# A two-layer decoder trunk on one core: a sixth pair of chunks by seven products, two chunks set aside, SiLU as one activation

## The chip, the core and the metric

The kernel runs on one core of one Trainium2 chip. The time is device microseconds of one execution. The program is written in a language in which every instruction is placed on an engine: PE (TensorE, matrix products), DVE (VectorE), ACT (ScalarE), POOL (GpSimd) and SP (SyncE, which here only issues transfers). Each engine runs its own instructions in the order in which the program lists them and waits on semaphores for the others.

## The reference

Two decoder layers over 256 tokens of width 1024. A layer is a token mixer and a SwiGLU sublayer, each followed by a residual and a layer norm. The change touches the second sublayer alone:

```python
D_FF = -(-8 * D_MODEL // (3 * 256)) * 256        # 2816

def swiglu(x, w_gate, w_up, w_down):
    return (jax.nn.silu(x @ w_gate) * (x @ w_up)) @ w_down

def reference(x, ...):
    for l in range(DEPTH):
        mix = hybrid_mixer(x, w_in[l], w_branch_sb[l], w_branch_moba[l], w_out[l])
        x = layer_norm(DEEPNORM_ALPHA * x + mix, ln_mix_g[l], ln_mix_b[l])
        ffn = swiglu(x, w_ffn_gate[l], w_ffn_up[l], w_ffn_down[l])
        x = layer_norm(DEEPNORM_ALPHA * x + ffn, ln_ffn_g[l], ln_ffn_b[l])
    return x
```

All inputs are float32.

## The kernel before

**Three products for one.** Every matrix is split into a high part of type float32r and a low part, the remainder. A product is `hi*hi + hi*lo + lo*hi`, three matrix instructions into one accumulator (`mm3`, L455; the instruction itself is recorded under L449). The weights come from memory in granules of 128x1024 float32 (512 KB). SP loads a granule into one of six `raw` tiles, ACT casts it into the ring `whi` (`CAST whi<-raw`, recorded under L57, the helper `act`), and DVE subtracts to get `wlo` (`TENSOR_TENSOR wlo<-raw,whi`, under L62, the helper `dve`). Both rings hold ten granules, so a granule can be split only once PE has used the one ten places ahead. In the mixer five granules a layer come by another way (`dma_line`, L183): POOL issues a load straight into `whi` (L187), ACT writes its negative into `wlo`, and POOL issues a second load that adds the weights onto it (L194).

**The second sublayer.** Its 2816 hidden features are 22 chunks of 128, numbered 0 to 21. Chunks 0 to 3 are made token by token (`h_line`, tiles `l0pft`, `l0sg`), and 4 to 21 feature by feature (`swiglu_line`, tiles `l0pf`, `l0sf`): ACT takes the sigmoid of the gate, DVE multiplies it by the gate and then by the other half, and the result is split into `h_hi` and `h_lo`. Then comes the down projection, whose stage the tiles `l0pd`, `l0ps`, `l0pt` (layer 1: `l1pd`, `l1pe`, `l1pt`) mark. For one chunk it takes a weight granule of 128x1024 and forms two token tiles by two halves of 512 columns: four results of three products each, 12 instructions.

**Pairs by seven products.** Two chunks together are a 2x2 block product, which the kernel does in the Strassen-Winograd way: seven products of blocks (21 instructions) in place of eight. For that, sums of the activations (`sums_line`: four additions on DVE of 128x128, then a split) and sums of the weights are needed. In the stream of weights a pair (p, q) is four steps: b (the granule of q, split whole), a (the granule of p, of which only the first half is split), then four sums of 128x512 that DVE makes in place in the two raw tiles, and t and u, which are these sums, each split whole. A chunk that is not in a pair is one step n. Accumulators `one`, `six`, `five`, `seven` (the tiles `ps` and `pt`; in layer 1 `ps` is a part of `pd`) collect products over all pairs; `combine_line` (L1070) afterwards adds them into the residual tiles x0 and x1 with eight DVE operations.

**What sets the order.** A planner in Python (`Weave`) keeps an estimate of each engine's time while the program is written, and lets side lines (splits, activations, norms) issue their next step when they are due. `DOWN` gives the order of chunks and pairs in the down projection. Its last eight entries (`HOLD`) are done for token tile 0 first, then for token tile 1, so that the norm of tile 0 can run beside the products of tile 1. `ASIDE` names chunks whose weights do not go through the rings: `put_aside` gives them a place in `xT_hi` and `xT_lo`, the transposed x, which is free once the last gate product has read it, and loads them there as `dma_line` does, except that the negative is made by POOL. Before, `ASIDE` is empty. The planner's entry for that POOL instruction is 0.3 us and a further 2.7.

Of the kernel before, what the change touches and what calls it, by code (L numbers as in the profile page):

```python
# [14 lines left out]
P = 128  # L15
DEPTH = 2
D = 1024
S = 256
# [10 lines left out]
NEG = -1e30  # L29
GCOLS = 1024  # L30
NG_LAYER = 122
DOWN = ((0, (4, 5), (6, 7), 1, (8, 9), 2, (10, 11), 3, (12, 13), 14, 15, 16, 17, 18, 19, 20, 21),
        (0, (4, 5), (6, 7), 1, (8, 9), 2, (10, 11), 3, (12, 13), 14, 15, 16, 17, 18, 19, 20, 21))
STEPS = [[e for d in down for e in
          ([("n", d)] if isinstance(d, int) else [("b", d[1]), ("a", d[0]), ("t", d[0]), ("u", d[0])])]
         for down in DOWN]
# [238 lines left out]
START = (("x00", 4.4), ("x10", 5.4), ("x01", 6.4), ("w10", 6.4), ("w11", 7.4), ("x11", 7.4), ("w20", 8.2), ("x02", 9.0),  # L275
         ("w21", 9.7), ("x12", 10.3), ("w30", 11.0), ("w31", 11.7))
BY_DMA = ((18, 23, 28, 33, 38), (18, 23, 28, 33, 38))
ASIDE = ((), ())
X_AFTER = {(2, 0): (0, 2), (2, 1): (1, 2)}
NSPLIT = 10  # L280
HOLD = 8
# [41 lines left out]
def hybrid_trunk_kernel(ctx: ExitStack, tc: tile.TileContext, w, xT_in, x_in, ln_in,  # L323
# [144 lines left out]
    def pe_done():  # L468
        return weave.t + HOP
# [336 lines left out]
    for l in range(DEPTH):  # L806
# [130 lines left out]

        def h_line(name, ps, j, t):
            sg = small_work(name, [P, 256])
            e = act(pe_done(), 256, nc.scalar.activation, sg, ps[:, :256], AF.Sigmoid)  # L940
            yield e
            dve(e, 256, nc.vector.tensor_mul, sg, sg, ps[:, :256])
            e = dve(e, 256, nc.vector.tensor_mul, sg, sg, ps[:, 256:])
            yield e + MARGIN
            tp = bankC(name + "T", [P, 2, P])
            pe_after(e)
            for i in range(2):
                transpose(tp[:, i, :], sg[:, i * P:(i + 1) * P])
            ts = slice(t * P, (t + 1) * P)
            e = pe_done()  # L950
            yield e
            yield from split_line(h_t[0][0][:, 2 * j:2 * j + 2, ts], h_t[0][1][:, 2 * j:2 * j + 2, ts], tp, 256, e)
# [5 lines left out]
        def sums_line(i, e):  # L958

            a, b = (raw_h.pop(c) for c in pairs[i])  # L960
            (a0, a1), (b0, b1) = ([x[:, t * P:(t + 1) * P] for t in range(2)] for x in (a, b))
            tmp = small_work(f"{L}hs{i}", [P, 4, P])
            for j, x, y, op in ((0, b1, a1, OP.subtract), (1, a0, tmp[:, 0], OP.add), (2, a0, a1, OP.subtract),
                                (3, b0, tmp[:, 1], OP.subtract)):
                e = dve(e, P, nc.vector.tensor_tensor, tmp[:, j], x, y, op=op)
            if i < 2:
                both = wide_work(f"{L}hw{i}", F32R).rearrange("p a h c -> p (a h c)")[:, :GCOLS]
            elif i < 4:
                both = work.tile([P, 2, 2, S], F32R, tag=("sbq", "sbk")[i - 2],
                                 name=f"{L}hw{i}").rearrange("p a h c -> p (a h c)")  # L970
            if i < 4:
                sums[i] = [both[:, n * 512:(n + 1) * 512].rearrange("p (j c) -> p j c", c=P) for n in range(2)]
            else:
                sums[i] = [x[:, 2:, :].rearrange("p k (j c) -> p (k j) c", c=P) for x in h_t[-1]]
            yield e
            yield from split_line(*sums[i], tmp, 512, e)

        def swiglu_line(name, ps, hi, lo, c):
            sg = small_work(name, [P, S])
            e = act(pe_done(), S, nc.scalar.activation, sg, ps[:, 0, :], AF.Sigmoid)  # L980
            yield e
            dve(e, S, nc.vector.tensor_mul, sg, sg, ps[:, 0, :])
            e = dve(e, S, nc.vector.tensor_mul, sg, sg, ps[:, 1, :])
            yield e
            if c in pair_of:
                i = pair_of[c]
                raw_h[c] = sg
                n = P if c == pairs[i][0] else S
                e = yield from split_line(hi[:, :n], lo[:, :n], sg[:, :n], n, e)
                if n == S:  # L990
                    yield from sums_line(i, e)
                return
            yield from split_line(hi, lo, sg, S, e)
# [53 lines left out]
        def seven_products(i, g):  # L1047

            a, b = pairs[i]
            (b_hi, b_lo), (a_hi, a_lo) = ws.take(g), ws.take(g + 1)  # L1050
            t0, t1 = slice(0, P), slice(P, S)
            one_, two_ = slice(0, 512), slice(512, GCOLS)
            (ha, la), (hb, lb) = h_parts(a), h_parts(b)
            s_hi, s_lo = sums[i]
            last = i == len(pairs) - 1
            into(c11, hb[:, t0], lb[:, t0], b_hi[:, one_], b_lo[:, one_])
            into(c12, s_hi[:, 3], s_lo[:, 3], b_hi[:, two_], b_lo[:, two_])
            ws.used(g)
            into(one, ha[:, t0], la[:, t0], a_hi[:, one_], a_lo[:, one_], last)
            ws.used(g + 1)  # L1060
            m_hi, m_lo = ws.take(g + 2)
            into(five, s_hi[:, 0], s_lo[:, 0], m_hi[:, one_], m_lo[:, one_], last)
            into(seven, s_hi[:, 2], s_lo[:, 2], m_hi[:, two_], m_lo[:, two_], last)
            ws.used(g + 2)
            m_hi, m_lo = ws.take(g + 3)
            into(six, s_hi[:, 1], s_lo[:, 1], m_hi[:, two_], m_lo[:, two_], last)
            into(c21, hb[:, t1], lb[:, t1], m_hi[:, one_], m_lo[:, one_])
            ws.used(g + 3)

        def combine_line(e):  # L1070

            v, r = (small_work(f"{L}{n}", [P, 512]) for n in ("pv", "pr"))
            x0, x1 = xs
            e = act(e, 512, nc.scalar.copy, v, six)
            yield e
            e = dve(e, 512, nc.vector.tensor_sub, v, one, v)
            residual(e, x0, halves[0], one)
            e = dve(e, 512, nc.vector.tensor_add, r, seven, v)
            e = dve(e, 512, nc.vector.tensor_add, v, five, v)
            residual(e, x0, halves[1], v, op=OP.subtract)  # L1080
            residual(e, x1, halves[0], r)
            e = dve(e, 512, nc.vector.tensor_add, r, five, r)
            residual(e, x1, halves[1], r, op=OP.subtract)

        g = G + NG_LAYER - NFC
        at = {}
        for n, d in enumerate(DOWN[l][:-HOLD]):
            if n == 6:
                late()
            if isinstance(d, int):  # L1090
                for t in range(2):
                    chunk(banks[t], g, d, t)
                ws.used(g)
                g += 1
                continue
            i = pairs.index(d)
            while i not in sums:
                weave.finish(swiglus)
            seven_products(i, g)
            g += 4  # L1100
            if i == len(pairs) - 1:
                combine = weave.start(combine_line(pe_done()))
        norms = []
        for t in range(2):
            def down(part, c0=NFC - HOLD, c1=NFC, first=False, last=True, t=t):
                for c in range(c0, c1):
                    chunk(part, g + c - NFC + HOLD, c, t, first and c == c0, last and c == NFC - 1)
                    if t == 1:
                        ws.used(g + c - NFC + HOLD)
                weave.finish([combine])  # L1110
# [91 lines left out]
```

## Time and profile before

| | before |
|---|---|
| runs, us | 720.8, 721.76 and a first one of 4118.94; median 721.76 |
| the profiled execution, us | 720.93 |
| its span, us | 719.2 |
| PE busy, share of the span | 710.8 us, 99% |
| DVE busy | 581.6 us, 81% |
| ACT busy | 407.9 us, 57% |
| POOL busy | 29.3 us, 4% |
| read from memory | 139.69 MB, 196 GB/s over the span |
| mean granted TensorE clock | 0.998 |

The span runs from the first to the last instruction of the program. A row of the timeline gives the start, the duration, the engine, the line of the kernel, the operation with its output and inputs (tile names without their numbers), and in brackets the idle time before it with what ended it. In a row of several instructions (x5) the duration is that of all together. A row of the list of waits gives who waited for whom.

### The profile page before, as it was taken

Reading aid. Unit: us, or ns where it says so; the run is one execution under the profiler, and the core shown is the slowest. Engines: PE = TensorE matmul, PEld = TensorE weight load, DVE = VectorE, ACT = ScalarE, POOL = GpSimd, SP = SyncE. Lnnn points to the kernel's source line nnn. Section 1 sums busy time; section 2 is a strip of 40 time slices with the busy share of each in tenths; the row PEclk is TensorE's granted clock in tenths of the full one; section 3 lists DMA queues with packets and bytes.
Section 4 is the critical chain, followed back from the end, with each engine's and each line's share of the span. In section 5 each row is a group of like instructions: output and inputs, shape, how many; then the busy total and the mean of one; then the engine's idle time right before and its main releaser. Section 6 shows DMA issues by size and latency. Waiting matters only on the chain.

```text
span 719.2 us, 12730 instructions
## 1 busy us (share of the span) xinstructions
PE 710.8 (99%) x5002; PEld 653.6 (91%) x5002; DVE 581.6 (81%) x871; ACT 407.9 (57%) x618; POOL 29.3 (4%) x50
## 2 busy tenths in 40 slices
PE   9999999999999999999999999999999999999995
PEld 7998999998899999988889989999888999998885
DVE  5988776698888777799877897778778877778986
ACT  6855676655565554557357557675446655544530
POOL 0000010000000000000000001000010000000001
PEclk9999999999999999999999999999999999999999
DMA  8986664367586564349459637636846865524731
GB/s 326 378 251 199 158 196 108 127 247 265 187 277 224 188 197 145 126 157 345 162 177 309 185 93 206 206 102 210 269 152 204 280 190 201 189 97 130 238 113 58
DMA packets 40668, 141.57 MB, mean 197 GB/s; under 512 B 4640, under 2 KB 5664, under 8 KB 40608
## 3 DMA queue, kind: packets, MB, share of 16 engines
q1 hardware_dynamic: 37152, 129.75, 53.6%
q0 software_dynamic: 2880, 10.49, 6.7%
q8 instruction: 39, 0.64, 0.3%
q10 hardware_dynamic: 576, 0.52, 0.2%
q14 instruction: 21, 0.17, 0.1%
HBM read 139.69 MB, written 1.05 MB: 196 GB/s over the span
## 4 chain that ended last, share of the span: by engine, by line
PE 99%; DVE 0%; POOL 0%; POOLq 0%; DVEq 0%; issue 0%
PE l1pf L449 14%; PE l0pf L449 14%; PE l0pg L449 6%; PE l1pg L449 6%; PE l0pd L449 6%; PE l1pd L449 4%; PE l0pk L449 3%; PE l1pk L449 3%; PE l0pq L449 3%; PE l0pft L449 3%; PE l1pft L449 3%; PE l1pvq L449 3%; PE l1pw L449 3%; PE l0pw L449 3%; PE l1pb L449 3%; PE l0pb L449 3%
## 5 line engine op out<-in xcount | busy, mean ns | idle before, releaser
L62 DVE TENSOR_TENSOR wlo<-raw,whi 128x1024 fp32r<-128x1024 f32 (+1 forms) x256 | 299.3, 1189 | 31.8 <-ACT whi L57 28.6
L57 ACT CAST whi<-raw 128x1024 fp32r<-128x1024 f32 (+1 forms) x256 | 256.9, 1023 | 60.9 <-DVE raw L62 25.0
L449 PE MATMUL l0pf<-xT_hi,whi 128*128 128x256 f32 x288 | 79.6, 276 | 0.0
L449 PE MATMUL l1pf<-xT_hi,whi 128*128 128x256 f32 x288 | 79.6, 276 | 0.0
L449 PE MATMUL l0pf<-xT_lo,whi 128*128 128x256 f32 x288 | 79.5, 276 | 0.0
L449 PE MATMUL l0pf<-xT_hi,wlo 128*128 128x256 f32 x288 | 79.5, 276 | 0.0
L449 PE MATMUL l1pf<-xT_lo,whi 128*128 128x256 f32 x288 | 79.5, 276 | 0.0
L449 PE MATMUL l1pf<-xT_hi,wlo 128*128 128x256 f32 x288 | 79.5, 276 | 0.0
L449 PEld LDWEIGHTS l1pf<-xT_lo,whi 128*128 128x128 f32 x288 | 54.1, 188 | 0.0
L449 PEld LDWEIGHTS l0pf<-xT_lo,whi 128*128 128x128 f32 x288 | 54.1, 188 | 0.0
L449 PEld LDWEIGHTS l0pf<-xT_hi,whi 128*128 128x128 f32 x288 | 54.1, 188 | 0.0
L449 PEld LDWEIGHTS l1pf<-xT_hi,whi 128*128 128x128 f32 x288 | 54.1, 188 | 0.0
L449 PEld LDWEIGHTS l0pf<-xT_hi,wlo 128*128 128x128 f32 x288 | 54.1, 188 | 0.0
L449 PEld LDWEIGHTS l1pf<-xT_hi,wlo 128*128 128x128 f32 x288 | 54.1, 188 | 0.0
L449 PE MATMUL l0pg<-xT_hi,whi 128*128 128x256 f32 x128 | 35.6, 279 | 0.0
L449 PE MATMUL l1pg<-xT_hi,whi 128*128 128x256 f32 x128 | 35.6, 278 | 0.0
L449 PE MATMUL l0pg<-xT_lo,whi 128*128 128x256 f32 x128 | 35.4, 276 | 0.0
L449 PE MATMUL l0pg<-xT_hi,wlo 128*128 128x256 f32 x128 | 35.4, 276 | 0.0
L449 PE MATMUL l1pg<-xT_lo,whi 128*128 128x256 f32 x128 | 35.4, 276 | 0.0
L449 PE MATMUL l1pg<-xT_hi,wlo 128*128 128x256 f32 x128 | 35.4, 276 | 0.0
L62 DVE TENSOR_TENSOR l1sf<-l1sf,l1pf 128x256 f32<-128x256 f32 x36 | 15.1, 421 | 15.4 <-ACT l1sf L57 14.7
L62 DVE TENSOR_TENSOR l0sf<-l0sf,l0pf 128x256 f32<-128x256 f32 x36 | 15.1, 421 | 11.9 <-ACT l0sf L57 11.2
(475 smaller groups left out, 1838.2 us busy)
## 6 DMA issues: line engine op xcount, KB each, us to landing
raw<-in_w_dram SPq DMA_DIRECT2D x230, 512.0 KB, 4.3
whi<-in_w_dram POOLq DMA_DIRECT2D x10, 512.0 KB, 4.3
wlo<-in_w_dram POOLq DMA_DIRECT2D x10, 512.0 KB, 7.2
ln<-in_ln_dram SPq DMA_DIRECT2D x8, 512.0 KB, 6.2
raw<-in_w_dram SPq DMA_DIRECT2D x8, 256.0 KB, 4.6
x<-in_x_dram SPq DMA_DIRECT2D x2, 512.0 KB, 8.2
out_dram<-x SPq DMA_DIRECT2D x3, 256.0 KB, 2.0
xT_raw<-in_xT_dram ACTq DMA_DIRECT2D x4, 128.0 KB, 4.5
```

What stands on the lines that cost most here:

```text
L57: f(*args, **kw)
L62: f(*args, **kw)
L449: nc.tensor.matmul(o, a, b, start=start, stop=stop)
```

## The change

The change has five parts, all in the second sublayer.

- `DOWN`: six pairs a layer in place of five; (14, 15) is new. The order changes too: five pairs stand first, then chunk 0, the sixth pair, chunk 1, and for the last eight chunks 2, 3 and 16 to 21, where it was 14 to 21.
- `ASIDE`: the weights of chunks 16 and 17 are loaded into the place of the transposed x.
- SiLU: one activation `Silu` on ACT, where it was a sigmoid on ACT and a multiplication on DVE.
- `sums_line`: a place for the sixth pair's sums (in free halves of the tiles of `h`).
- `combine_line`: its eight operations are issued in four pieces with at least 3.2 us of the planner's time between them. The ln parameters of the second norm are loaded one entry earlier (`n == 5`).

```diff
-DOWN = ((0, (4, 5), (6, 7), 1, (8, 9), 2, (10, 11), 3, (12, 13), 14, 15, 16, 17, 18, 19, 20, 21),
+DOWN = (((4, 5), (6, 7), (8, 9), (10, 11), (12, 13), 0, (14, 15), 1, 2, 3, 16, 17, 18, 19, 20, 21),
...
-ASIDE = ((), ())
+ASIDE = ((16, 17), (16, 17))
...
         def h_line(name, ps, j, t):
             sg = small_work(name, [P, 256])
-            e = act(pe_done(), 256, nc.scalar.activation, sg, ps[:, :256], AF.Sigmoid)
+            e = act(pe_done(), 256, nc.scalar.activation, sg, ps[:, :256], AF.Silu)
             yield e
-            dve(e, 256, nc.vector.tensor_mul, sg, sg, ps[:, :256])
             e = dve(e, 256, nc.vector.tensor_mul, sg, sg, ps[:, 256:])
...
             if i < 4:
-                sums[i] = [both[:, n * 512:(n + 1) * 512].rearrange("p (j c) -> p j c", c=P) for n in range(2)]
+                places = [[both[:, n * 512:(n + 1) * 512].rearrange("p (j c) -> p j c", c=P) for n in range(2)]]
+            elif i == 4:
+                places = [[x[:, 2:, :].rearrange("p k (j c) -> p (k j) c", c=P) for x in h_t[-1]]]
+            elif i == 5:
+                places = [[x[:, 0::2, P:] for x in h_t[k]] for k in (1, 2)]
             else:
-                sums[i] = [x[:, 2:, :].rearrange("p k (j c) -> p (k j) c", c=P) for x in h_t[-1]]
+                places = [[x[:, 6:, :].rearrange("p k (j c) -> p (k j) c", c=P) for x in (xT_hi, xT_lo)]]
+            n = 4 // len(places)
+            sums[i] = [[hi_lo[m][:, j] for hi_lo in places for j in range(n)] for m in range(2)]
             yield e
-            yield from split_line(*sums[i], tmp, 512, e)
+            for k, hi_lo in enumerate(places):
+                e = yield from split_line(*hi_lo, tmp[:, k * n:(k + 1) * n], n * P, e)
 
         def swiglu_line(name, ps, hi, lo, c):
             sg = small_work(name, [P, S])
-            e = act(pe_done(), S, nc.scalar.activation, sg, ps[:, 0, :], AF.Sigmoid)
+            e = act(pe_done(), S, nc.scalar.activation, sg, ps[:, 0, :], AF.Silu)
             yield e
-            dve(e, S, nc.vector.tensor_mul, sg, sg, ps[:, 0, :])
             e = dve(e, S, nc.vector.tensor_mul, sg, sg, ps[:, 1, :])
...
             e = dve(e, 512, nc.vector.tensor_sub, v, one, v)
             residual(e, x0, halves[0], one)
+            yield weave.t + 3.2
             e = dve(e, 512, nc.vector.tensor_add, r, seven, v)
             e = dve(e, 512, nc.vector.tensor_add, v, five, v)
+            yield weave.t + 3.2
             residual(e, x0, halves[1], v, op=OP.subtract)
             residual(e, x1, halves[0], r)
+            yield weave.t + 3.2
             e = dve(e, 512, nc.vector.tensor_add, r, five, r)
             residual(e, x1, halves[1], r, op=OP.subtract)
...
-            if n == 6:
+            if n == 5:
                 late()
...
-                    chunk(part, g + c - NFC + HOLD, c, t, first and c == c0, last and c == NFC - 1)
+                    chunk(part, g + c - NFC + HOLD, DOWN[l][c - NFC], t, first and c == c0, last and c == NFC - 1)
```

The order of the instructions at three places follows. On DVE in layer 0's down stage, a raw tile's number is the step's number in the stream of weights. Before, from the t of the pair (8, 9) to the t of the pair (10, 11):

```order
L62 TENSOR_TENSOR wlo_91<-raw111_3297,whi_89 128x1024
L62 TENSOR_TENSOR wlo_91<-raw110_3173,whi_89 128x1024
L62 TENSOR_TENSOR wlo_91<-raw114_3299,whi_89 128x1024
L62 TENSOR_TENSOR wlo_91<-raw115_3423,whi_89 128x1024
L62 TENSOR_TENSOR wlo_91<-raw116_3425,whi_89 128x512
L62 TENSOR_TENSOR raw116_3425<-raw116_3425 128x512
L62 TENSOR_TENSOR raw116_3425<-raw116_3425,raw115_3423 128x512
L62 TENSOR_TENSOR raw115_3423<-raw115_3423,raw116_3425 128x512
L62 TENSOR_TENSOR raw115_3423<-raw115_3423 128x512
L62 TENSOR_TENSOR wlo_91<-raw116_3425,whi_89 128x1024
```

Now, on the same engine, from the t of the pair (10, 11) to the t of the pair (12, 13):

```order
L62 TENSOR_TENSOR wlo_91<-raw113_3273,whi_89 128x1024
L62 TENSOR_TENSOR wlo_91<-raw112_3271,whi_89 128x1024
L62 TENSOR_TENSOR wlo_91<-raw116_3395,whi_89 128x1024
L62 TENSOR_TENSOR wlo_91<-raw117_3397,whi_89 128x512
L62 TENSOR_TENSOR raw117_3397<-raw117_3397 128x512
L62 TENSOR_TENSOR raw117_3397<-raw117_3397,raw116_3395 128x512
L62 TENSOR_TENSOR raw116_3395<-raw116_3395,raw117_3397 128x512
L62 TENSOR_TENSOR raw116_3395<-raw116_3395 128x512
L62 TENSOR_TENSOR wlo_91<-raw117_3397,whi_89 128x1024
```

The whole split of the plain chunk (raw114) that stood between two pairs is gone from this place; one pair's t and u are followed at once by the next pair's b and a.

On POOL, between the first norm of layer 0 (`l0a_ve`) and its second (`l0b_ve`), as one piece of the difference:

```order
 L67 TENSOR_TENSOR l0a_ve_2061<-l0a_ve_2061,few 128x1
-L67 TENSOR_SCALAR l0b_ve_3775<-l0b_ve_3775 128x1
-L67 TENSOR_TENSOR l0b_ve_3775<-l0b_ve_3775,few 128x1
-L67 TENSOR_SCALAR l0b_ve_3866<-l0b_ve_3866 128x1
-L67 TENSOR_TENSOR l0b_ve_3866<-l0b_ve_3866,few 128x1
+L187 DMA xT_hi<-in_w_dram 128x1024 x2
+L67 TENSOR_SCALAR xT_lo<-xT_hi 128x1024 x2
+L194 DMA xT_lo<-in_w_dram 128x1024 x2
+L67 TENSOR_SCALAR l0b_ve_3765<-l0b_ve_3765 128x1
+L67 TENSOR_TENSOR l0b_ve_3765<-l0b_ve_3765,few 128x1
```

Six instructions are new on POOL's queue: two loads, two multiplications of 128x1024 by -1, and two adding loads.

On ACT in layer 1, at the first activation of the second sublayer (`l1sg00`, which reads the gate product `l1pft00`), before:

```order
L57 CAST whi_89<-raw193_5647 128x1024
L57 ACTIVATE l1pw1_5700,l1a_ve1_5781<-x1_88,l1a_nmu1_5780 128x1024
L57 ACTIVATE l1sg00_5829<-l1pft00_5804 128x256
L57 CAST whi_89<-raw194_5657 128x1024
L57 CAST xT_hi_85<-l1a_tp10_5838 128x4x128
L57 CAST whi_89<-raw195_5664 128x1024
```

And now:

```order
L57 CAST whi_89<-raw195_5637 128x1024
L57 ACTIVATE l1pw1_5690,l1a_ve1_5771<-x1_88,l1a_nmu1_5770 128x1024
L57 ACT_TABLE_LOAD
L57 ACTIVATE l1sg00_5819<-l1pft00_5794 128x256
L57 CAST whi_89<-raw196_5647 128x1024
L57 CAST xT_hi_85<-l1a_tp10_5828 128x4x128
```

A load of the activation table stands between the norm's square and the first SiLU (the raw tiles' numbers are two higher, since the stream of layer 0 has two steps more). The new order has such a load in both layers at this place and one more ahead of layer 1's first sigmoid (`l1sb0_kb0`). In layer 1 the table load carries the wait for PE's product, and in layer 0 it carries no wait.

More of the change, by code (lines that the diff above doesn't have):

```diff
@@ L31 @@
 NG_LAYER = 122
-DOWN = ((0, (4, 5), (6, 7), 1, (8, 9), 2, (10, 11), 3, (12, 13), 14, 15, 16, 17, 18, 19, 20, 21),
-        (0, (4, 5), (6, 7), 1, (8, 9), 2, (10, 11), 3, (12, 13), 14, 15, 16, 17, 18, 19, 20, 21))
+DOWN = (((4, 5), (6, 7), (8, 9), (10, 11), (12, 13), 0, (14, 15), 1, 2, 3, 16, 17, 18, 19, 20, 21),
+        ((4, 5), (6, 7), (8, 9), (10, 11), (12, 13), 0, (14, 15), 1, 2, 3, 16, 17, 18, 19, 20, 21))
 STEPS = [[e for d in down for e in
@@ L1056, in seven_products @@
             into(c11, hb[:, t0], lb[:, t0], b_hi[:, one_], b_lo[:, one_])
-            into(c12, s_hi[:, 3], s_lo[:, 3], b_hi[:, two_], b_lo[:, two_])
+            into(c12, s_hi[3], s_lo[3], b_hi[:, two_], b_lo[:, two_])
             ws.used(g)
@@ L1061, in seven_products @@
             m_hi, m_lo = ws.take(g + 2)
-            into(five, s_hi[:, 0], s_lo[:, 0], m_hi[:, one_], m_lo[:, one_], last)
-            into(seven, s_hi[:, 2], s_lo[:, 2], m_hi[:, two_], m_lo[:, two_], last)
+            into(five, s_hi[0], s_lo[0], m_hi[:, one_], m_lo[:, one_], last)
+            into(seven, s_hi[2], s_lo[2], m_hi[:, two_], m_lo[:, two_], last)
             ws.used(g + 2)
             m_hi, m_lo = ws.take(g + 3)
-            into(six, s_hi[:, 1], s_lo[:, 1], m_hi[:, two_], m_lo[:, two_], last)
+            into(six, s_hi[1], s_lo[1], m_hi[:, two_], m_lo[:, two_], last)
             into(c21, hb[:, t1], lb[:, t1], m_hi[:, one_], m_lo[:, one_])
```

## The prediction

> **What bounds the kernel now.** I read the page first: busy times, then the chain that ended last.
>
> ```profile
> span 719.2 us, 12730 instructions
> PE 710.8 (99%) x5002; PEld 653.6 (91%) x5002; DVE 581.6 (81%) x871; ACT 407.9 (57%) x618; POOL 29.3 (4%) x50
> PE 99%; DVE 0%; POOL 0%; POOLq 0%; DVEq 0%; issue 0%
> ```
>
> A busy TensorE is not yet a TensorE at its peak, so the second view is that of the waits, for TensorE alone (columns: microseconds in total, times, longest). One row answers, from the start of the program:
>
> ```profile
> PE busy L407 <- DVE few L404: 0.9, 1, 0.9
> ```
>
> The third view is the chain in order of time (start, duration, what):
>
> ```profile
> 301.59 4.10 PE l0pd L449 x18
> ...
> 328.13 4.76 PE l0pd L449 x21
> ...
> 335.61 17.68 PE l0pd L449 x78
> ...
> 655.13 1.39 PE l1pd L449 x6
> ...
> 710.32 1.45 PE l1b_rest L449 x12
> 713.03 0.78 POOL l1b_ve L67
> ```
>
> 17.68/78 and 4.76/21 are both 0.2267 us: the 512-column products of the down projection follow each other without a gap. So the span is the sum of the products plus a tail after 711.8. Whatever removes a product gains 0.2267 us, as long as the split weights come in time. Who splits them is read from VectorE's timeline in layer 0's down stage, which begins at 301.59; the window row ahead of it has, after the stretch, the sum, then PE, PEld, DVE, ACT, POOL, clock, DMA share, GB/s:
>
> ```profile
> 311.00:316.00 5.00, 5.00 (x24) 4.14 (x23) 4.93 (x6) 2.74 (x4) 0.00 (x0) 1.00 0.67 220
> ```
>
> ```profile
> 302.10 0.87 DVE L62 TENSOR_TENSOR l0sf<-l0sf,l0pf 128x256 f32<-128x256 f32 x2 [1.00 <-ACT l0sf L57]
> ...
> 307.32 0.69 DVE L62 TENSOR_TENSOR raw<-raw 128x512 f32<-128x512 f32 x1
> ...
> 310.11 5.36 DVE L62 TENSOR_TENSOR wlo<-raw,whi 128x1024 fp32r<-128x1024 f32 x5
> ...
> 318.29 5.38 DVE L62 TENSOR_TENSOR wlo<-raw,whi 128x1024 fp32r<-128x1024 f32 x5
> ...
> 326.49 7.05 DVE L62 TENSOR_TENSOR wlo<-raw,whi 128x1024 fp32r<-128x1024 f32 x6
> ```
>
> VectorE works 4.93 us of 5 here: it is nearly a second bound. Six splits in 7.05 are 1.17 apiece. The four weight sums of a pair take 310.11 - 307.32 = 2.79. From 310.11 to 318.29, 8.18 us, lies one pair (four sums, three whole splits, one half) and one plain chunk; the pair alone is 8.18 - 1.17 = 7.01. TensorE needs 21 x 0.2267 = 4.76 for a pair, 12 x 0.2267 = 2.72 for a plain chunk: a pair costs VectorE 2.25 more than it gives TensorE, a plain chunk 1.55 less.
>
> **Products.** One pair more per layer: 24 products become 21. Six fewer in all, 6 x 0.2267 = **-1.36 us**. This is all that the change takes from TensorE.
>
> **Order of the chunks.** Before, plain chunks stand between the pairs; now five pairs come first. Whether VectorE keeps up is an account in layer 0. At 302.10 it begins the last SwiGLU product (one, 0.42, where two stood: group row below). By the new order there follow the half split of the third pair (0.61), one h_lo (0.35), four sums: the third pair's t split begins at 302.10 + 0.42 + 0.61 + 0.35 + 2.79 = 306.3. The fourth's begins at 313.3, the fifth's (12, 13) at 320.3, and after a plain chunk the sixth's (14, 15) at 320.3 + 8.18 = 328.5; each ends 1.2 later, at 321.5 and 329.7. TensorE wants the fifth's t at 301.59 + 4 x 4.76 + 9 x 0.2267 = 322.7, the sixth's at 301.59 + 5 x 4.76 + 2.72 + 2.04 = 330.2. VectorE is **1.2 and then 0.5 us ahead**: no wait, but cover of half a microsecond. Anything that holds VectorE longer in 302 to 328 appears on TensorE, in both layers.
>
> ```profile
> L62 DVE TENSOR_TENSOR l0sf<-l0sf,l0pf 128x256 f32<-128x256 f32 x36 | 15.1, 421 | 11.9 <-ACT l0sf L57 11.2
> ```
>
> **The chunks set aside.** Two splits a layer leave ScalarE and VectorE (in the account already: 16 and 17 are never split there). In their place POOL issues a load, multiplies 128x1024 by -1 from xT_hi to xT_lo, and issues an adding load.
>
> ```profile
> whi<-in_w_dram POOLq DMA_DIRECT2D x10, 512.0 KB, 4.3
> wlo<-in_w_dram POOLq DMA_DIRECT2D x10, 512.0 KB, 7.2
> ```
>
> Issued at about 301.6, when TensorE leaves xT, the loads land near 306, and after two multiplications the adding ones near 317. TensorE wants chunk 16 at 301.59 + 6 x 4.76 + 2 x 2.72 + 2 x 1.36 = 338.3: 21 us of cover. What the multiplications do to VectorE, whose sums and splits run beside them, no row shows: POOL has done nothing of this size. The nearest rows:
>
> ```profile
> 0.72 0.42 POOL L401 MEMSET ends<- 128x384 f32 x1 [0.29 <-POOLq L1188]
> 1.20 0.10 POOL L402 MEMSET ends<- 128x2 f32 x1
> ```
>
> ```profile
> 350.19 0.75 POOL L67 TENSOR_SCALAR l0b_ve<-l0b_ve 128x1 f32<-128x1 f32 x1 [165.15 <-ACT l0pd L57]
> 351.02 0.94 POOL L67 TENSOR_TENSOR l0b_ve<-l0b_ve,few 128x1 f32<-128x1 f32 x1
> ```
>
> ```profile
> 350.13 1.42 DVE L62 SCALAR_TENSOR_TENSOR x<-x,l0b_nmu,ln 128x512 f32<-128x512 f32 x2 [1.37 <-ACT l0pd L57]
> 351.99 1.41 DVE L62 SCALAR_TENSOR_TENSOR x<-x,l0b_ve,ln 128x512 f32<-128x512 f32 x2 [0.44 <-POOL l0b_ve L67]
> ```
>
> The memsets give 0.32/382 = 0.84 ns an element, 0.86 us for 1024; with the 0.75 of a one-element TENSOR_SCALAR the multiplication lasts some 1.61 (an estimate; the kernel's own planner allows 3.0). VectorE's pair took 1.42 beside POOL's instructions and 1.41 alone: the fixed 0.75 costs it nothing, on the elements nothing is shown. So VectorE loses between 0 and 3.0 us an instruction. I take 0.86, the element part, the middle one of the priced cases: two of them, 1.72, less 0.5 of cover, are 1.22 a layer, **+2.44 us**. The Trainium skill, page "SBUF — State Buffer", section "SBUF: two separate sides", speaks against the change: VectorE and GpSimd share a port pair, and a VectorE instruction with two SBUF inputs and a GpSimd one that reads SBUF shut each other out for the whole instruction. The 1.42 beside 1.41 contradicts "whole" for one-element instructions; by the rule the sum would hold 1.61 twice, which is a rival below.
>
> **SiLU as one activation.** 22 products of 0.42 a layer leave VectorE, 9.2 us; since TensorE waited for none, they buy only the lead counted above. But the new order shows three ACT_TABLE_LOADs more.
>
> ```profile
> 118.10 0.64 ACT L57 COPY l0mb_o_low<-l0mb_o 64x256 f32<-64x256 f32 x2
> 118.75 1.28 ACT L57 ACT_TABLE_LOAD   x1
> ...
> 185.38 0.39 ACT L57 ACTIVATE l0sg<-l0pft 128x256 f32<-128x256 f32 x1 [2.20 <-PE l0pft L449]
> 538.98 0.38 ACT L57 ACTIVATE l1sg<-l1pft 128x256 f32<-128x256 f32 x1 [2.25 <-PE l1pft L449]
> ```
>
> ```profile
> L57 ACT ACTIVATE l1sb_kb<-l1sb_s 128x768 f32<-128x768 f32 x8 | 5.8, 818 | 2.5 <-DVE l1sb_s L62 2.5
> ```
>
> A load is 1.28. Layer 0's waits for nothing and fits into the 2.20 idle; the one back to sigmoid ahead of l1sb_kb likewise meets idle time. Layer 1's stands behind the wait for TensorE's product, so SiLU starts at 540.26 and two weight casts queue behind it.
>
> ```profile
> 542.48 1.22 DVE L62 TENSOR_TENSOR wlo<-raw,whi 128x1024 fp32r<-128x1024 f32 x1
> ```
>
> ```profile
> 542.74 4.80 PE l1pft L449 x21
> ```
>
> The second of these casts ends near 542.95 (0.28, 0.95, 0.49, 0.95 and waits behind 540.26), and VectorE, which must first finish the split before it and an xT_lo, splits it at about 543.4 instead of 542.48, to 544.6; TensorE wants it at 542.74 + 7 x 0.2267 = 544.3. That is 0.3 at least, 1.28 at most: I take **+0.5**. The Trainium skill, page "ScalarE: Activation LUTs", section "What ACT_TABLE_LOAD costs", adds 1.38 us of drain to the load's 1.28; here the load begins 0.01 after the copy ahead of it ends, so the row disagrees. By the page the sum would be about 1.4 more.
>
> **The combination in pieces** is the same eight operations, with weight splits between them, beside 8 x 1.36 = 10.9 us of products of the first token tile. VectorE stood ready 0.34 ahead of the norm's first operand:
>
> ```profile
> 347.21 0.69 DVE L62 SCALAR_TENSOR_TENSOR x<-x,l0pd 128x512 f32<-128x512 f32 x1 [0.34 <-PE l0pd L449]
> ```
>
> Its stage grows by 7.01 - 4 x 1.17 = 2.3 while TensorE's shrinks by 0.68, so the norm may start up to 2.7 late; the second tile's 10.9 us lie between. In layer 0 I take **+0.4** (0 to 2.7) for the next layer's first splits; in layer 1 the tail follows the last products either way.
>
> **The sum.** The profiled execution took 720.93 (719.2 of span, 1.73 around it), 0.8 under the median of the runs shown, 721.76. 720.93 - 1.36 + 2.44 + 0.5 + 0.4 = **722.9 us**.
>
> **Rivals.** (A) POOL's multiplications cost VectorE nothing: 720.93 - 1.36 + 0.9 = 720.5, and 719.6 if the 0.9 is covered too. For it speaks the 1.42 beside 1.41; against it, that those POOL instructions touched one element a partition. (B) VectorE stands still for the whole instruction: 2 x (2 x 1.61 - 0.5) = 5.4, 725.9; with the planner's 3.0 each 2 x 5.5 = 11, 731.5. (C) The other way round: VectorE, which has no pause, keeps POOL out until its first real gap.
>
> ```profile
> 336.80 2.49 DVE L62 TENSOR_TENSOR wlo<-raw,whi 128x1024 fp32r<-128x1024 f32 x2 [0.66 <-ACT whi L57]
> ```
>
> From about 336, two multiplications and the adding load (7.2) end at 346.4, against 338.3 wanted: 8.1 a layer, 720.5 + 16.2 = 736.7, slower by 2%. It decides once POOL's last multiplication ends after 331.1, and passes 2% at 338.6. Against it: the sums wait for each other and leave gaps at every step.
>
> **Chances.** Forecast with (B) as far as 2.26 us an instruction (721.5 to 728.5): 0.48; (A): 0.38; a longer hold (to 735): 0.10; (C): 0.02; something not seen: 0.02. The range 719.5 to 728.5 leaves out the long hold, (C), the unseen and a little of (A). About 2% (14.4 us) is what a measurement of this kernel can tell from no change; only (C) or an unseen stall reaches it, and no gain here does: faster 0.01, within 2% 0.96, slower 0.03.
>
> **What would show it.** In the new profile: 21 products at 0.2267 in each of six pairs; TensorE's waits name wlo on VectorE ahead of l0pt and l1pt, in the fifth and sixth pair; VectorE's wlo and raw rows between 305 and 310 are longer by what POOL's TENSOR_SCALAR xT_lo lasts; a short wait in l1pft behind the table load. No such wait, and rows of unchanged length, mean (A). A wait ahead of chunk 16 means (C). I am wrong if TensorE waits where none of this stands, or if VectorE's round is not 7.01 when pairs follow each other.

## The result

| | before | after |
|---|---|---|
| median of six runs of each, side by side, us | 720.82 | 724.53 (724.1 to 725.48) |
| ratio to before, 95% interval | 1 | 1.0054 (1.0044 to 1.0065) |
| the profiled execution, us | 720.93 | 724.1 |
| its span, us | 719.2 | 722.3 |
| PE busy, us | 710.8 | 711.7 |
| DVE busy, us | 581.6 | 571.8 |
| POOL busy, us | 29.3 | 47.3 |

One of the six runs of before is a first one of 4118.94, which the ratio leaves out. The changed kernel is 0.54% slower: measurably so, and within 2%. The forecast was 722.9, with a range of 719.5 to 728.5.

### The profile page after: what moved, and what is told of

Read it like the earlier page. It is cut to its first block, busy times and chain, and to the rows that moved or that the text cites. A ratio compares the mean times of both kernels' runs of the same rounds, so it can differ in the third digit from the quotient of the medians.

```text
span 722.3 us, 12634 instructions
## 1 busy us (share of the span) xinstructions
PE 711.7 (99%) x4996; PEld 651.8 (90%) x4996; DVE 571.8 (79%) x847; ACT 408.4 (57%) x625; POOL 47.3 (7%) x62
## 5 line engine op out<-in xcount | busy, mean ns | idle before, releaser
L57 ACT ACTIVATE l1sf<-l1pf 128x256 f32<-128x256 f32 x18 | 6.9, 383 | 35.7 <-PE l1pf L449 35.7
L449 PEld LDWEIGHTS l0pg<-xT_hi,whi 128*128 128x128 f32 x128 | 24.0, 188 | 0.4
```

What stands on the lines that cost most here:

```text
L57: f(*args, **kw)
L449: nc.tensor.matmul(o, a, b, start=start, stop=stop)
```

## The profile after

Span, busy times, and shares of the chain that ended last, from the page of the changed kernel:

```profile
span 722.3 us, 12634 instructions
...
PE 711.7 (99%) x4996; PEld 651.8 (90%) x4996; DVE 571.8 (79%) x847; ACT 408.4 (57%) x625; POOL 47.3 (7%) x62
...
PE 43%; DVE 4%; issue 1%; ACT 1%; POOL 0%; POOLq 0%; DVEq 0%; ACTq 0%
```

TensorE has six products fewer in the trace (x5002 before), and VectorE is 9.8 us less busy. Neither shortened the span. VectorE is now on the chain, where it had 0%. (The chain is followed back only as far as 366 us, so these shares add up to about half of the span.)

The waits of TensorE in the changed kernel (us in total, times, longest):

```profile
PE busy L407 <- DVE few L404: 0.9, 1, 0.9
PE l0pt L449 <- DVE wlo L62: 0.8, 2, 0.4
PE l1pt L449 <- DVE wlo L62: 0.7, 2, 0.4
PE l0b_tp L462 <- DVE x L62: 0.5, 1, 0.5
```

Before, only the first row stood there. Two waits a layer at `l0pt` and `l1pt` are those that the prediction named. They stand in layer 0 at the fifth and the sixth pair; TensorE's timeline:

```profile
322.48 0.39 PE L449 MATMUL l0pt<-whi,l0h_hi 128*128 128x512 f32 x1
323.21 0.50 PE L449 MATMUL l0pt<-wlo,l0h_hi 128*128 128x512 f32 x1 [0.35 <-DVE wlo L62]
323.55 0.39 PE L449 MATMUL l0pt<-whi,l0h_lo 128*128 128x512 f32 x1
...
330.60 0.39 PE L449 MATMUL l0pt<-whi,l0h_hi 128*128 128x512 f32 x1
331.41 0.50 PE L449 MATMUL l0pt<-wlo,l0h_hi 128*128 128x512 f32 x1 [0.42 <-DVE wlo L62]
331.75 0.39 PE L449 MATMUL l0pt<-whi,l0h_lo 128*128 128x512 f32 x1
```

The step to a product's successor is 0.2267 as a rule. Here it is 0.73 and 0.81, and each time the next step is 0.34 too. The two places lose (0.73 + 0.34 + 0.81 + 0.34) - 4 x 0.2267 = 1.31 us; the rest of the 1.49 that layer 0's stage loses in the table below is spread over other steps of it.

POOL and VectorE in the same stretch of the changed kernel. POOL's timeline first, its second multiplication once more by itself:

```profile
305.93 6.19 POOL L67 TENSOR_SCALAR xT_lo<-xT_hi 128x1024 fp32r<-128x1024 f32 x2 [3.56 <-DMA xT_hi<-in_w_dram]
308.99 3.13 POOL L67 TENSOR_SCALAR xT_lo<-xT_hi 128x1024 fp32r<-128x1024 f32 x1
```

VectorE's timeline, with one split beside POOL and one later also shown by itself (the x4 and x5 rows include them):

```profile
306.28 2.06 DVE L62 TENSOR_TENSOR wlo<-raw,whi 128x1024 fp32r<-128x1024 f32 x1
306.28 5.77 DVE L62 TENSOR_TENSOR wlo<-raw,whi 128x1024 fp32r<-128x1024 f32 x4
314.88 4.24 DVE L62 TENSOR_TENSOR wlo<-raw,whi 128x1024 fp32r<-128x1024 f32 x4
321.94 5.37 DVE L62 TENSOR_TENSOR wlo<-raw,whi 128x1024 fp32r<-128x1024 f32 x5
323.21 1.22 DVE L62 TENSOR_TENSOR wlo<-raw,whi 128x1024 fp32r<-128x1024 f32 x1
330.13 4.77 DVE L62 TENSOR_TENSOR wlo<-raw,whi 128x1024 fp32r<-128x1024 f32 x4
```

A multiplication lasts 3.1 us on POOL. Beside the first, one split lasts 2.06 in place of 1.22: 0.84 more. The four splits of the round last 5.77 in place of 4.24: 1.53 for two multiplications, and from there on everything on VectorE is that much later. Layer 1 has the same 5.77.

Two more places lose time. Whole stages are compared by the first and last start of one group of products (min, median and max duration in ns stand ahead of them), here of the products of `l1pvq` (first stage of layer 1) and `l1pft` (token by token part of layer 1's second sublayer). Before:

```profile
L449 PE MATMUL l1pvq<-whi,xT_hi x32: 389/389/477, 358.8 to 381.3; 128*128 128x512 f32 x32
L449 PE MATMUL l1pft<-whi,xT_hi x32: 389/389/478, 533.3 to 556.0; 128*128 128x512 f32 x32
```

After:

```profile
L449 PE MATMUL l1pvq<-whi,xT_hi x32: 388/389/478, 359.6 to 383.1; 128*128 128x512 f32 x32
L449 PE MATMUL l1pft<-whi,xT_hi x32: 389/389/477, 535.0 to 558.3; 128*128 128x512 f32 x32
```

`l1pvq` takes 23.5 in place of 22.5 and `l1pft` 23.3 in place of 22.7. From the starts of single products, at two decimals, these are 0.96 and 0.56. The same starts give the whole ledger, after against before:

| stretch | predicted | measured |
|---|---|---|
| products | -1.36 | -1.36 |
| waits in layer 0's and layer 1's down stage | +2.44 | 1.49 + 1.36 = +2.85 |
| handover from layer 0 to layer 1 | +0.4 | +0.96 |
| table load in layer 1 | +0.5 | +0.56 |
| tail, and what differs at the start | 0 | +0.16 |
| span | +1.98 | +3.17 |

(The last row but one is what is left of 3.17. The spans are 719.2 and 722.3 on the page; 3.17 is the difference of the two executions, 724.1 and 720.93.)

## The experiments

The theory after these traces: three separate stalls ate the 1.36. POOL's multiplications hold VectorE for a time that goes by their elements; the load of SiLU's table delays two casts in layer 1; and VectorE comes late to the norm of the second token tile. For the last, POOL's hold was at first thought to be half of the cause, and the spacing of the combination only after **slot**.

### POOL's multiplications: moved to ScalarE, doubled, halved, replaced

**slot.** The negative is made by ScalarE, between the casts for a and for t of the fourth and fifth pair, and POOL multiplies nothing:

```diff
         if self.aside(g):
-            e = weave.pool(weave.t, nc.gpsimd.tensor_scalar, lo, hi.bitcast(F32), -1.0, None, op0=OP.mult) + 2.7
+            self.negate.append(g)
+            while g in self.negate:
+                yield weave.t + 0.1
+            e = self.negated
...
                 if what == "t" and self.negate:
+                    n_hi, n_lo = self.parts[self.negate.pop(0)]
+                    self.negated = weave.act(0.0, GCOLS, nc.scalar.mul, n_lo, n_hi.bitcast(F32), -1.0)
```

> The changed kernel (724.5 us), except that the negative of the two chunks set aside is written by ACT, each in the idle time between the casts of a and of t of the fourth and fifth pair, and no longer by POOL. Theory (POOL's element part, 0.84 us an instruction, holds VectorE, and the cover of 0.5 us a layer is too small for two of them): the four splits of 2.05 us return to 1.22; TensorE's waits ahead of l0pt and l1pt, 1.49 and 1.36 us of lost time, fall to 0.3 or less; the wait of 0.95 at the start of layer 1 falls to about 0.5, because VectorE reaches the norm sooner; the 0.56 at the table load stays. Time 721.1 to 721.9. Rival (the order of the pairs alone is too dense for VectorE): the waits ahead of l0pt and l1pt stay over 1 us a layer, time 723.8 to 724.8.

Measured: 720.74, ratio to before 1.0000 (0.9991 to 1.0009). The waits at `l0pt` and `l1pt` are gone. The same place on VectorE, then one of ScalarE's two new instructions a layer, in this kernel:

```profile
306.08 4.22 DVE L62 TENSOR_TENSOR wlo<-raw,whi 128x1024 fp32r<-128x1024 f32 x4
```

```profile
308.67 1.06 ACT L57 ACTIVATE xT_lo<-xT_hi 128x1024 fp32r<-128x1024 f32 x1
```

4.22 in place of 5.77, and the same sweep takes ScalarE 1.06. So the multiplications on POOL, and not the longer run of pairs, caused the waits in the down stage. Of the 3.15 us between the two profiled executions (724.1 and 720.95) 2.86 lie in the two down stages, as much as the ledger has there. The time came out a little under what was expected. One part of the expectation missed: the handover to layer 1, which was to lose 0.5, still loses 0.86, so POOL's hold is not what delays it.

**twice.** POOL multiplies each granule twice (the second overwrites the first with the same values).

```diff
             e = weave.pool(weave.t, nc.gpsimd.tensor_scalar, lo, hi.bitcast(F32), -1.0, None, op0=OP.mult) + 2.7
+            e = weave.pool(weave.t, nc.gpsimd.tensor_scalar, lo, hi.bitcast(F32), -1.0, None, op0=OP.mult) + 5.4
```

> The changed kernel with each of POOL's multiplications issued twice (the second writes the same values again). Theory (each holds VectorE for its element part, 0.84 us): two more splits of 2.05 us a layer, 1.68 us a layer on VectorE and, since no cover is left, on TensorE: 3.4 us more, about 727.9. Rival (each holds VectorE for all of its 3.1 us, and what is seen is what cover left over): 6.2 a layer, 737. Second rival (the long splits have nothing to do with POOL): no change, 724.5.

Measured: 728.25, close to the theory's 727.9. POOL's row, and VectorE's sum beside the first of the four:

```profile
305.83 12.27 POOL L67 TENSOR_SCALAR xT_lo<-xT_hi 128x1024 fp32r<-128x1024 f32 x4 [3.23 <-DMA xT_hi<-in_w_dram]
```

```profile
305.90 1.52 DVE L62 TENSOR_TENSOR raw<-raw 128x512 f32<-128x512 f32 x1
```

Here the first instruction met is a sum of 128x512, which takes 0.69 as a rule: 1.52 is 0.83 more. The hold does not depend on how long VectorE's own instruction is. POOL is busy for 12.27 us, and VectorE loses four times some 0.8 in them (0.72 to 0.89), not 12.27: rival (B) falls.

**halves.** Each multiplication is made as two of 128x512.

```diff
-            e = weave.pool(weave.t, nc.gpsimd.tensor_scalar, lo, hi.bitcast(F32), -1.0, None, op0=OP.mult) + 2.7
+            for h in (slice(0, 512), slice(512, 1024)):
+                e = weave.pool(weave.t, nc.gpsimd.tensor_scalar, lo[:, h], hi[:, h].bitcast(F32), -1.0, None, op0=OP.mult) + 2.7
```

> The changed kernel with each of POOL's multiplications made as two of 128x512. What is open is whether the 0.84 us by which one VectorE instruction is longer beside each POOL instruction is a share of its length (it equals the 0.86 that the memset rows gave for 1024 elements) or a price of each instruction. Theory 'by elements', as the prediction had it: four lengthened VectorE instructions a layer of about +0.42 each, the same 1.7 in all, 724.0 to 724.8. Rival 'a fixed price': four of +0.84 each, waits at l0pt and l1pt of 1.3 to 1.4 as where POOL multiplied twice, 727.5 to 728.5.

Measured: 724.86, at the upper end of the theory. POOL's row, then VectorE's, the first split again also by itself:

```profile
306.02 6.59 POOL L67 TENSOR_SCALAR xT_lo<-xT_hi 128x512 fp32r<-128x512 f32 x4 [3.40 <-DMA xT_hi<-in_w_dram]
```

```profile
306.52 1.63 DVE L62 TENSOR_TENSOR wlo<-raw,whi 128x1024 fp32r<-128x1024 f32 x1
306.52 5.75 DVE L62 TENSOR_TENSOR wlo<-raw,whi 128x1024 fp32r<-128x1024 f32 x4
```

The split is 0.41 longer (1.63 against 1.22), half of 0.84, and the round is as long as with two whole ones (5.75 and 5.77). This settles the form: the hold goes with the size of POOL's sweep, 0.84/1024 = 0.82 ns an element, whatever the grouping; it is no price of an instruction (the rival's 727.5 and more did not come). Whether it follows the elements or the instruction's length can't be told apart here, since the length halves too: 3.1 for 1024 elements, 1.6 for 512, so the hold is about a quarter of it both times.

**memset.** POOL fills xT_lo with zeros instead, so the low part of chunks 16 and 17 leaves out the subtraction of the high part.

```diff
-            e = weave.pool(weave.t, nc.gpsimd.tensor_scalar, lo, hi.bitcast(F32), -1.0, None, op0=OP.mult) + 2.7
+            e = weave.pool(weave.t, nc.gpsimd.memset, lo.bitcast(F32), 0.0) + 2.7
```

> The changed kernel, with POOL filling xT_lo with zeros in place of multiplying xT_hi by -1 (so the low part of chunks 16 and 17 leaves out the subtraction of the high part). The instruction writes the same 128x1024 but reads nothing from SBUF, and need not wait for the load of xT_hi. Theory 'any sweep of POOL over SBUF holds VectorE': one VectorE instruction beside each is still longer by some 0.8, the waits at l0pt and l1pt stay, about 724 us. Rival 'what holds is the reading' (the Trainium skill, page SBUF — State Buffer, section SBUF: two separate sides, speaks of a GpSimd instruction that reads SBUF): VectorE's rows have their usual lengths, the waits at l0pt and l1pt go, and the time is that of the kernel with the negative on ScalarE, 720.7 to 721.5.

Measured: 720.95. POOL, then VectorE beside it:

```profile
301.91 1.87 POOL L67 MEMSET xT_lo<- 128x1024 f32 x2
```

```profile
302.09 0.69 DVE L62 TENSOR_TENSOR wlo<-raw,whi 128x512 fp32r<-128x512 f32 x1
...
303.03 0.68 DVE L62 TENSOR_TENSOR raw<-raw 128x512 f32<-128x512 f32 x1
...
305.81 4.22 DVE L62 TENSOR_TENSOR wlo<-raw,whi 128x1024 fp32r<-128x1024 f32 x4
```

The waits at `l0pt` and `l1pt` are gone, and VectorE's splits and sums beside the two fills have their usual lengths. A sweep that writes 128x1024 and reads nothing cost VectorE nothing; the theory that any sweep holds it falls. The fill is also shorter (0.93 against 3.1) and runs earlier, beside other instructions, since it need not wait for the load: what is shown is that the reading sweep holds and this one does not, not that reading alone is the difference.

The Trainium skill, page "SBUF — State Buffer", section "SBUF: two separate sides", names both conditions: a GpSimd instruction that reads SBUF against a VectorE one with two SBUF inputs. Five kernels here agree on POOL's side of it (multiplications hold; fills do not, and neither do ScalarE's copies); VectorE's side is not tested, since every instruction that was held here has two inputs. On the amount it says that the one shuts the other out for the whole instruction. The trace does not agree: the split that began at 306.28 ended at 308.34, while POOL's first multiplication ran from 305.93 to 308.99 (spans on POOL are rough, but the two together are 6.19 and four are 12.27).

### The table load

**warm.** Ahead of the first token tile's products a SiLU over one column loads the table early.

```diff
             weave.finish(norms[:t + 1])
+            if t == 0:
+                nc.scalar.activation(warm, zero, AF.Silu)
             pe_after(xT_ready[t])
```

> The changed kernel with one more activation, a SiLU of one column, issued on ACT before the first gate product of each layer, so that the table load stands in ACT's idle time and not behind the wait for TensorE's product. Theory (the load in layer 1 costs the 0.56 us by which l1pft falls behind): the delay of l1pft is 0, time 723.8 to 724.1. Rival (l1pft falls behind for the norm, not for the load): the delay stays at 0.56, time 724.5.

Measured: 723.76, ratio to before 1.0042 (1.0027 to 1.0058), 0.77 under the changed kernel's median. The two intervals overlap, so the total settles nothing, and the stage must. ScalarE of the changed kernel, then of this one:

```profile
540.68 1.28 ACT L57 ACT_TABLE_LOAD   x1 [2.24 <-PE l1pft L449]
541.98 0.38 ACT L57 ACTIVATE l1sg<-l1pft 128x256 f32<-128x256 f32 x1
```

```profile
538.15 1.28 ACT L1004 ACT_TABLE_LOAD   x1
539.45 0.20 ACT L1004 ACTIVATE warm<-few 128x1 f32<-128x1 f32 x1
540.39 0.38 ACT L57 ACTIVATE l1sg<-l1pft 128x256 f32<-128x256 f32 x1 [0.74 <-PE l1pft L449]
```

The load now lies in the 2.24 us in which ScalarE waited for TensorE, and the first SiLU starts 1.59 earlier. `l1pft` of this kernel takes 22.7 again:

```profile
L449 PE MATMUL l1pft<-whi,xT_hi x32: 388/389/479, 534.7 to 557.4; 128*128 128x512 f32 x32
```

So the 0.56 in that stage is the table load, and an early load removes it.

**silu_only.** The kernel before, with SiLU as one activation (the three lines of the diff on `h_line` and `swiglu_line`) and nothing else.

> The kernel before, with SiLU as one activation and nothing else of the change. Theory: TensorE waited for none of the 22 products a layer that go, so they are worth nothing here, and the table load ahead of layer 1's first SiLU costs its 0.5 to 0.6: 721.3 to 721.5 against 720.8. Rival: VectorE, busy 4.93 of 5 us in the down stage, gives its 9.2 us a layer back somewhere: 720.5 or less.

Measured: 722.13, above both expectations. The end of the chain of before, and of this kernel:

```profile
715.74 0.40 DVE x L62
```

```profile
715.77 0.40 DVE x L62
```

VectorE's last instruction stands at the same place, so 1.14 of the 1.17 by which the span is longer lies behind it, between the last store's issue and the end of the program; nothing in the trace says why. One run can't tell whether this comes again, so neither expected total is settled by it. Ahead of it the stages read as the theory has them: `l1pft` takes 23.3 (22.7 before), the table load once more.

```profile
L449 PE MATMUL l1pft<-whi,xT_hi x32: 387/389/481, 532.8 to 556.1; 128*128 128x512 f32 x32
```

The row's first start is 0.5 earlier than before, but so is the first product of the mixer at 17 us (16.59 against 17.06), ahead of any SiLU: a difference between executions. The 22 products a layer that VectorE no longer makes show up nowhere as a gain.

**sigm.** The changed kernel, with the sigmoid and VectorE's product back.

```diff
-            e = act(pe_done(), 256, nc.scalar.activation, sg, ps[:, :256], AF.Silu)
+            e = act(pe_done(), 256, nc.scalar.activation, sg, ps[:, :256], AF.Sigmoid)
             yield e
+            dve(e, 256, nc.vector.tensor_mul, sg, sg, ps[:, :256])
```

> The changed kernel with the sigmoid and VectorE's product back. Theory: without the lead of 0.42 that the last product gave VectorE at the start of the down stage, and with the h tiles split later, the fifth and sixth pair come later by 0.42 and more: 0.8 us or more a layer above the changed kernel, less 0.56 for the table load that goes: 725.0 to 727.5. Rival: the products had slack here too, as in the kernel before, and only the table load goes: 724.0.

Measured: 726.71, as the theory had it: 2.2 above the changed kernel, though the 0.56 of the table load is gone. TensorE's waits in it, the three largest:

```profile
PE l0b_tp L462 <- DVE x L62: 1.4, 2, 0.8
PE l0pt L449 <- DVE wlo L62: 1.1, 2, 0.7
PE l1pt L449 <- DVE wlo L62: 1.1, 2, 0.8
```

Each of them was 0.5 to 0.8 in the changed kernel. SiLU as one activation was worth nothing in the kernel before and some 2 us net here, because here VectorE is late already.

### The last eight chunks and the handover

**noaside.** `ASIDE` is empty; chunks 16 and 17 go through the rings.

```diff
-ASIDE = ((16, 17), (16, 17))
+ASIDE = ((), ())
```

> The changed kernel with ASIDE empty: chunks 16 and 17 go through the rings, POOL multiplies nothing. Theory: the waits at the fifth and sixth pair (1.4 a layer) go, but VectorE has two splits more, 2 x 1.2 a layer, in the stretch in which it also has the combination's eight operations, and TensorE waits in the last eight chunks or at the norm: 3 to 5 us a layer less the 1.4, so 727 to 731. Rival: the setting aside buys nothing; the last chunks' splits find room, and the time is 721.0 to 722.

Measured: 727.5. In both layers the waits move to where the last eight chunks stand; the row of layer 0:

```profile
PE l0pd L449 <- DVE wlo L62: 1.8, 3, 0.8
```

The setting aside is needed: two splits a layer more cost more than POOL's hold does.

**onepiece.** The combination in one piece (the three `yield weave.t + 3.2` taken out).

> The changed kernel with the combination's eight operations in one piece. Theory: eight operations of about 0.69 are 5.5 us in which VectorE splits nothing, against 1.36 of products per chunk and tile; with the splits 1 or 2 chunks ahead TensorE waits 2 to 3.5 a layer in l0pd and l1pd: 728 to 731. Rival: the rings hold enough split weights (chunks 16 and 17 are ready aside), nothing waits: 724.3, or less by up to 0.9 since the norm of tile 0 can start sooner.

Measured: 730.86. One wait a layer, as long as the theory's; the row of layer 0:

```profile
PE l0pd L449 <- DVE wlo L62: 2.9, 1, 2.9
```

Behind this wait TensorE also ran slower in layer 0. Its steps are 0.43 in place of 0.23 for some 2.7 us, and the granted clock (behind POOL's column in the row) is 0.50:

```profile
342.00:343.00 1.00, 1.00 (x4) 0.71 (x3) 1.00 (x2) 0.95 (x1) 0.00 (x0) 0.50 0.84 311
```

Behind the equal wait in layer 1 this did not happen. About 1.35 of the 730.86 are this lowered clock, whose cause is open, and not the price of the one piece.

The handover of this kernel loses nothing, though POOL multiplies here as in the changed one; but the wait of 2.9 also gave VectorE time to catch up.

**slot_warm** joins **slot** and **warm**.

> Both edits together: the negative on ACT in its idle time, and the SiLU table loaded early. Theory: the six products fewer (1.36 us) remain as a gain, against the rest of the wait at layer 1's start and a tail 0.2 longer; 720.3 to 721.2, a ratio of 0.9993 to 1.0005 to the kernel before (720.8). Rival (other waits take the place of those removed): above 721.8.

Measured: 720.58, ratio 0.9997 (0.9988 to 1.0005). The list of TensorE's waits has only the one at the start of the program, but 0.43 is still lost between the layers.

**sw_y16.** **slot_warm** with the pieces of the combination 1.6 apart (the line stands three times).

```diff
-            yield weave.t + 3.2
+            yield weave.t + 1.6
```

> Both stalls out (the negative on ScalarE, SiLU's table loaded early), and the combination's pieces at least 1.6 instead of 3.2 us of the planner's time apart. With 3.2 the run without both stalls still lost 0.44 us between the last product of layer 0 and the first of layer 1, and took 720.58. Theory: that loss comes from the spacing, which puts the last piece of the combination, and behind it the norm of token tile 1, behind weight splits on VectorE; with 1.6 it goes: about 720.1 us, ratio to before about 0.999, the first layer's handover 0.0 to 0.1. Rival: the loss comes from the longer stage on VectorE (2.3 us a layer more than before), wherever the pieces stand: 720.6, handover 0.4. Second rival: pieces closer together delay the splits between them and TensorE waits in the last eight chunks: 721 or more, with a wait at l0pd or l1pd.

Measured: 719.56, ratio 0.9981 (0.9972 to 0.9990): faster than both kernels, by 0.19% than before and, from the two ratios (1.0054/0.9981), by 0.7% than the changed one. It came out under the 720.1 that was expected. Its handover, against that of **slot_warm**, from which it differs by the spacing alone:

```profile
L456 PE MATMUL l1pvq<-whi,xT_hi x32: 389/389/477, 357.5 to 380.0; 128*128 128x512 f32 x32
```

```profile
L456 PE MATMUL l1pvq<-whi,xT_hi x32: 388/389/477, 358.2 to 381.2; 128*128 128x512 f32 x32
```

22.5 (as before) against 23.0. VectorE's first residual of token tile 1 in the changed kernel, with no idle time ahead of it, and TensorE's last product for it:

```profile
361.45 0.68 DVE L62 SCALAR_TENSOR_TENSOR x<-x,l0pd 128x512 f32<-128x512 f32 x1
```

```profile
359.35 0.39 PE L449 MATMUL l0pd<-whi,l0h_lo 128*128 128x512 f32 x1
```

and the same two in **sw_y16**:

```profile
358.14 0.68 DVE L62 SCALAR_TENSOR_TENSOR x<-x,l0pd 128x512 f32<-128x512 f32 x1
```

```profile
357.30 0.39 PE L456 MATMUL l0pd<-whi,l0h_lo 128*128 128x512 f32 x1
```

2.10 from the start of the last product to the residual, and 0.84 here. The spacing of 3.2 made VectorE late for the norm, and the rival, that the longer stage itself costs 0.4, falls: the work is the same here.

How the spacing does it stands earlier in VectorE's timeline, in the changed kernel:

```profile
341.27 2.46 DVE L62 TENSOR_TENSOR wlo<-raw,whi 128x1024 fp32r<-128x1024 f32 x2 [1.57 <-ACT whi L57]
```

The weights of this split have not come: the cast that it waits for starts at 340.18, when ScalarE has itself waited 4.12 for their load. The last two pieces of the combination are issued behind the split, so VectorE stands idle with work at hand. With 1.6 all eight operations are done by 340.24, ahead of the late split, and there is no such idle time. The runs with 3.2 and the same order of instructions at this place lose the more, the longer the idle time is (**halves** departs, and its stage ahead of the handover is 0.6 longer than the changed kernel's):

| run | idle ahead of this split | lost in the handover |
|---|---|---|
| halves | 2.19 | 0.97 |
| twice | 1.68 | 0.99 |
| changed kernel | 1.57 | 0.96 |
| slot | 1.46 | 0.86 |
| warm | 1.28 | 0.75 |
| memset | 1.28 | 0.70 |
| slot_warm | 1.01 | 0.43 |
| sw_y16 | none | 0.00 |

So **slot** and **slot_warm**, whose instructions are the same here, differ by when a load landed, and POOL's hold has little part in the handover. Why the load is late was not tested; in the changed kernel the two loads of the ln parameters, which the change issues one entry earlier, stand right ahead of it in SP's queue (332.63 and 333.55).

Of the 1.0 us between the medians of **slot_warm** and **sw_y16** only this 0.43 is shown to be the spacing. In the profiled executions 0.69 more lies ahead of the first product of the mixer, and 0.40 is lost again in layer 1's mixer, as in **twice** and **memset**; the cause of either is open.

## Why the prediction was right, and where it was short

**What bounds the kernel, and the products: right.** TensorE's products follow at 0.2267, six fewer, -1.36.

**VectorE's account and its cover: right to 0.1.** It put the t split of the fifth pair at 320.3 and of the sixth at 328.5, plus the hold. With the round's 1.53 these are 321.8 and 330.0; the rows say 321.94 and 330.13. A round of VectorE without POOL beside it, from 314.88 to 321.94, takes 7.06, for the 7.01 that it named. It had TensorE want the sixth's t at 330.2; TensorE came to it at 331.41, 1.21 late. The step said 1.22.

**POOL's hold: the size right by luck, the reason wrong.** VectorE's rows are longer and TensorE waits where the prediction said, so rivals (A) and (C) fall. But 0.86 was the middle one of several priced cases, and no row showed it. It was called the element part of an instruction of 1.61, from the rate of two fills. The multiplication takes 3.1, and 1.6 for half the elements, so nearly all of it is element part: had VectorE been held for that, the 3.0 case of rival (B), 731.5, would have been the time. And fills, which gave the rate, did not hold VectorE at all in **memset**. That 0.84 was measured, close to 0.86, is not explained by the step. The sign "longer by what POOL's TENSOR_SCALAR xT_lo lasts" did not come either: 0.84 beside 3.1. Why the hold is this share of the sweep stays open.

**A term that was missing: the restart.** Behind each of the four waits TensorE's next step is 0.34 in place of 0.23, 0.11 each time, 0.44 in all. Of the 2.85 in the two down stages the waits themselves are 2.16, less than the 2.44 of the sum (two holds lengthen the round by 1.53, not 1.72), the restarts 0.44, and 0.25 is spread over other steps.

**The table load: right**, 0.56 for 0.5, by the mechanism given (two casts queued behind it). The load starts as soon as TensorE's product releases it, and SiLU follows its end within 0.02 us. The "short wait in l1pft" has no row in the list of TensorE's waits; the stage's length shows it.

**The handover: the place right, the mechanism wrong.** The step "In layer 0 I take +0.4 (0 to 2.7)" measured 0.96. It counted the growth of VectorE's stage against TensorE's. That growth stands in **sw_y16** too, where the handover loses nothing. What decides is the pause of 3.2 between pieces, which puts the last two behind a split that waits for its load.

Of the 1.2 by which the sum (722.9) fell short of the profiled execution (724.1), 0.56 is the handover, 0.41 the down stages, 0.06 the table load and 0.16 the ends. So the answer, no difference of 2%, came from the steps given, though the sizes of POOL's hold and of the handover did not come from the reasons given for them. The direction stood in the sum too, at half the size: slower by 0.27% (722.9 against 720.93), where 0.54% was measured.

## What to carry to other kernels

Where VectorE is nearly as busy as TensorE, a change is priced by how late it makes VectorE at the next operand that TensorE wants, not by busy time: here 9.8 us less of VectorE bought nothing, and 1.5 us of hold at one place cost more than the products gave. An elementwise sweep with time to spare goes to an engine whose idle time lies there and which does not hold VectorE, and a function's table is loaded in a wait that exists anyway. Work that is cut into pieces to let other work through still has a due date for its last piece, and a piece that is issued behind an instruction whose data may come late waits with it.

## What was not expected of the hardware

- POOL's multiplication of 128x1024 lasts 3.1 us where ScalarE's takes 1.06, and yet VectorE is held only for 0.84 of it. Whether 3.1 is its length without VectorE beside it wasn't tried.
- The hold falls on one VectorE instruction and in one piece: a sum of 0.69 became 1.52, a split of 1.22 became 2.06.
- After each of the four short waits TensorE needed 0.11 us more for the step behind the first product, 0.44 in all. After one wait of 2.9 (**onepiece**, layer 0) it ran at a granted clock of 0.50 for some 2.7 us, and after another of the same length (layer 1) it did not.
- Two executions can differ by 0.8 us by the first product of `l0pq` in the mixer (16.46 to 17.27 in these traces) and by 1.1 us behind VectorE's last instruction, so single runs settle waits and stages here, and not totals under a microsecond.
